# The second scan's elementwise work with one operand in PSUM on VectorE

## The chip, the core and the metric

The kernel runs on one core of a Trainium2 chip. The metric is the device time of one execution in microseconds (us). A core has engines that each work through a queue of their own, in order: TensorE (PE in the profile, its weight loads PEld) multiplies matrices, VectorE (DVE), ScalarE (ACT) and GpSimd (POOL) do the elementwise work, SyncE (SP) starts most transfers. An instruction waits in its queue until what it reads is there and what it overwrites is free; all that stands behind it on that engine waits with it. SBUF is the on-chip memory, PSUM the memory into which TensorE writes and which the other engines can read and write too.

## The reference

Two layers run one after the other on x of 1024 rows by 1024 columns, in float32. The first is a hybrid block (an S5 scan, attention over selected keys, gates). The second is a block of which one half is attention with three dilations and the other half a Mamba-2 scan; their outputs are gated, normalised, joined, multiplied by a matrix and normalised once more. The change lies in the Mamba-2 scan alone. Cut to what matters (16 heads of 64 columns, in 2 groups of 8; 8 chunks of 128 rows; state of 128):

```python
xg = (x * dt[..., None])                      # by chunk
a_cs = jnp.cumsum(dt * a, axis=-1)            # within a chunk
decay = jnp.exp(segsum(adt))                  # exp(a_cs[l] - a_cs[s]), 0 above the diagonal
cb = jnp.einsum('bclgn,bcsgn->bcgls', cc, bc)
y_diag = jnp.einsum('bcgjls,bcsgjp->bclgjp', cb[:, :, :, None] * decay, xg)
decay_to_end = jnp.exp(a_cs[..., -1:] - a_cs)
states = jnp.einsum('bcsgn,bcsgjp->bcgjpn', bc, xg * decay_to_end)
# the states are carried from chunk to chunk: h * chunk_decay + states, prev is h before the chunk
y_off = jnp.einsum('bclgn,bcgjpn->bclgjp', cc, prev) * jnp.exp(a_cs)
y = y_diag + y_off
```

## The kernel before, in words

The program is not written in the order in which it runs. Python generators (tasks) describe the work; a planner (the class `Sched`) plays them in planned time, with a cost for each kind of instruction and a priority for each task, and so fixes the order of each engine's queue. Every instruction is recorded by one helper, so that all of them carry line L280, and a row is told by the names of its tiles. A pair of engines in `yield (G..., V...)` means that the planner takes the one that it thinks is done first. A tile pool hands out a fixed number of buffers: a task that asks for a buffer with none free stands still until one is released.

Most of the time TensorE multiplies: the two large products of each layer (names g<-m,wh and g<-m,wl). A weight block comes by DMA into `raw`, ScalarE rounds it into `wh`, GpSimd takes the rest, `wl = raw - wh`, and TensorE multiplies by both; there are two buffers each of raw, and two pairs of wh and wl (numbers wh_76 with wl_77, wh_78 with wl_79). During the second scan, from about 1089 to 1310 us of the span, these products (the projections of the second layer) fill TensorE between the scan's own matmuls, and their results are read out of PSUM as zp (gates) or go through a convolution on VectorE (names cr, ac, xs).

The scan (`ssd_core`, `chunk`) goes through two groups of heads, first 0, then 1, with the convolution of group 1's inputs between them. For each of the 8 chunks of a group four tasks run beside one another:

- `rows`: four transposes (t<-cst,xs) into a PSUM buffer b, then xg = transposed x times dt, on VectorE.
- `decay`: a DMA fetches R, the cumulated a_cs of 8 heads, to all 128 partitions (R has two buffers); 8 VectorE instructions (E<-R,nacs,cst) make E = R - a_cs plus a mask for each head; ScalarE takes exp; a matmul puts C times B into PSUM (t<-CT,BT), VectorE multiplies E by it (E<-E,t).
- `off`: ScalarE takes exp of R, GpSimd multiplies it by C (R<-R,CT).
- `state`: GpSimd makes xd = xg times the decay to the chunk's end, and the old state times the chunk's decay (pv<-pv,eend); a matmul (s<-xd,Br) makes the chunk's part, VectorE adds it (pv<-pv,s).

Then 16 matmuls (o<-E,xg and o<-R,pv) make the chunk's output, and VectorE adds the skip (xs<-xs,dsk,o, four rows). The buffer of R comes free when these matmuls are done, so the fetch for chunk c+2 starts behind the output of chunk c. `gate_ssm` and `gate_mix` multiply the outputs by the gates and sum their squares (sq<-sq,xs); the task that finishes the eighth block also forms the norm.

Of the kernel before, what the change touches and what calls it, by code (L numbers as in the profile page):

```python
# [311 lines left out]
class Kernel:  # L312
# [5 lines left out]
    def run(self, upto):  # L318
# [12 lines left out]
        def nm(base):  # L331
            cnt[0] += 1
            return f"{base}_{cnt[0]}"
# [41 lines left out]

        cst = pC.tile([128, 912], F32, name="cst")
        ident, tri, cm2 = cst[:, 0:128], cst[:, 128:256], cst[:, 256:512]
        selB, ones, negT = cst[:, 512:640], cst[:, 640:768], cst[:, 768:896]
        eye = cst[:, 896:912]
        gs = pC.tile([128, 16], F32, name="gs")  # L380
        sc = pC.tile([128, 8], F32, name="sc")
# [119 lines left out]
        X = {}  # L501
# [1232 lines left out]
        def gate_mix(u, half, k, done):  # L1734

            r = half * 1024 + k * 128
            yield Q.dma_start(mix_d[r:r + 128], u)
            fire(mix_ev[half][k])
            sq, prev, mine = X["sq"], sq_last[half], Ev()
            sq_last[half] = mine  # L1740
            if prev is None:
                yield A.activation(sq, u, AF.Square)
            else:
                yield A.activation(u, u, AF.Square)
                yield prev
                yield (G.tensor_tensor(sq, sq, u, op=OP.add), V.tensor_tensor(sq, sq, u, op=OP.add))
            fire(mine)
            fire(done)
            count_mix[half] += 1
            if count_mix[half] == 8:  # L1750
                b = yield TB
                yield [P.matmul(b[:, t:t + 1], sq[:, t * 128:(t + 1) * 128], ones[:, 0:1], start=True, stop=True) for t in range(8)]
                ss = X["c2"].tile([128, 8], F32, name=nm("ssm"))
                yield V.tensor_copy(ss, b[:, 0:8])
                release(TB, b)
                rstd[half] = yield from rsqrt(X["c2"], ss, 8, 1.0 / 1024, 1e-5, "m")
                fire(rstd_ev[half])

        count_mix = [0, 0]

# [33 lines left out]
        def ssd_prep():  # L1794
# [33 lines left out]
            yield V.tensor_scalar(X["nacs"], b[:, 0:128], -1.0, None, op0=OP.mult)  # L1828
            yield V.tensor_tensor(X["dec"], b[:, 128:256], X["nacs"], op=OP.add)
            yield A.activation(X["dec"], X["dec"], AF.Exp)  # L1830
            yield A.activation(X["eend"], b[:, 128:256], AF.Exp)
            release(TB, b)
            fire(ssd_ev)
# [88 lines left out]
        def chunk(g, c, xs, prev, pv_ev):  # L1922
# [1 line left out]
            cs = slice(c * 128, (c + 1) * 128)  # L1924
            hs = slice(c * 16 + 8 * g, c * 16 + 8 * g + 8)
            dt2 = X["dt"].rearrange("p c h -> p (c h)")
            xg_ev, e_ev, r_ev = Ev(), Ev(), Ev()
            T = {}

            def bc(ap, n=64):  # L1930
# [2 lines left out]
            def rows():  # L1933
                T["xg"] = yield X["xg"]
                b = yield TB
                yield [P.transpose(b[:, k * 128:(k + 1) * 128], xs[k][:, cs], ident) for k in range(4)]
                yield V.tensor_tensor(T["xg"], b.rearrange("p (h d) -> p h d", h=8), bc(dt2[:, hs]), op=OP.mult)
                release(TB, b)
                fire(xg_ev)

            def decay():

                R = yield X["R"]
                E = yield X["E"]
                T["R"], T["E"] = R, E
                yield Q.dma_start(R, acs_d[hs].rearrange("(o h) l -> o h l", o=1).to_broadcast([128, 8, 128]))
                yield [V.scalar_tensor_tensor(E[:, h], R[:, h], X["nacs"][:, c * 16 + 8 * g + h:c * 16 + 8 * g + h + 1], negT, op0=OP.add, op1=OP.add)
                       for h in range(8)]
                spawn(off(R), 50 + c)
                yield A.activation(E, E, AF.Exp)  # L1950
                b = yield TB
                yield P.matmul(b[:, 0:128], BT[:, cs], CT[:, cs], start=True, stop=True)
                yield V.tensor_tensor(E, E, b[:, None, 0:128].to_broadcast([128, 8, 128]), op=OP.mult)
                release(TB, b)
                fire(e_ev)

            def off(R):
                if c:
                    yield A.activation(R, R, AF.Exp)
                    yield G.tensor_tensor(R, R, CT[:, None, cs].to_broadcast([128, 8, 128]), op=OP.mult)  # L1960
                fire(r_ev)

            def state():
                yield xg_ev
                xd = yield X["xd"]
                yield G.tensor_tensor(xd, T["xg"], bc(X["dec"][:, hs]), op=OP.mult)
                if c:
                    yield pv_ev[c - 1]
                nx = yield X["pv"]
                if c:  # L1970
                    yield G.tensor_tensor(nx, prev[c - 1], bc(X["eend"][:, hs]), op=OP.mult)
                b = yield SB
                sb = b
                yield P.matmul(sb, Br[:, c], xd.rearrange("p h d -> p (h d)"), start=True, stop=True)
                release(X["xd"], xd)
                s3 = sb.rearrange("p (h d) -> p h d", h=8)
                if c:
                    yield V.tensor_tensor(nx, nx, s3, op=OP.add)
                else:
                    yield V.tensor_copy(nx, s3)  # L1980
                release(SB, b)
                prev[c] = nx
                fire(pv_ev[c])
# [354 lines left out]
```

## Time and profile before

| what | value |
|---|---|
| times of the runs | 2014.16, 2019.17, 2019.45 us, median 2019.17 |
| profiled execution | 2019.02 us, its span 2017.3 us |
| mean granted clock of TensorE | 0.989 |
| busy: PE / VectorE / ScalarE / GpSimd | 1937.5 / 1369.6 / 803.8 / 624.9 us |

The span is the time from the first to the last recorded instruction; 1.7 us lie around it. [...] Busy times of different engines overlap. A row's own duration can reach into the next one's, since an engine starts an instruction before the one in front has fully ended. "Idle before" is time in which the engine stood still just before a row, with the engine or transfer that ended it.

### The profile page before, as it was taken

The page shows a single profiled execution, that of the slowest core. Times are in us where ns is not written, and L with a number is a line of the kernel's source. Part 1 is how long each engine was busy: PE and PEld are TensorE (multiplying, and loading weights), DVE is VectorE, ACT ScalarE, POOL GpSimd, SP SyncE. Part 2 cuts the span into 40 slices and gives each one's busy share as a digit, 9 for nine tenths or more (in the row PEclk, how much of TensorE's full clock was granted, in tenths as well). Part 3 has the DMA queues.
Part 4 walks back from the last instruction along what each step waited for, and adds up shares of the span by engine and source line. Part 5 has one row for each costly group of instructions (what it writes and reads, how often), then busy time and mean ns, then how long its engine had stood idle before and what let it go on. Part 6 is the DMA issues. An engine that isn't in the chain of part 4 may idle for free. (4 is left out here: it accounts for less than half of the span.)

```text
span 2017.3 us, 32636 instructions
## 1 busy us (share of the span) xinstructions
PE 1937.5 (96%) x12477; PEld 1634.6 (81%) x12477; DVE 1369.6 (68%) x3203; ACT 803.8 (40%) x1420; POOL 624.9 (31%) x435
## 2 busy tenths in 40 slices
PE   6999999999998999999999899999999999979997
PEld 4777877778887888998887677788889878869997
DVE  5899999986558754635357887746665666684348
ACT  5563322222357742214122333336554555673310
POOL 2215788872300012312223534530100100111233
PEclk9999999999999999999999999999999999989999
DMA  8213466658534134624322334361223311246622
GB/s 287 53 51 86 126 180 166 171 167 274 167 104 152 53 123 139 210 68 114 84 72 83 98 114 128 108 213 53 85 74 92 97 53 64 74 126 196 217 70 84
DMA packets 279004, 245.91 MB, mean 122 GB/s; under 512 B 47376, under 2 KB 230208, under 8 KB 278848
## 3 DMA queue, kind: packets, MB, share of 16 engines
q1 hardware_dynamic: 277696, 239.64, 39.0%
q0 software_dynamic: 1152, 4.19, 0.6%
q8 instruction: 98, 1.61, 0.3%
q14 instruction: 58, 0.48, 0.1%
HBM read 173.46 MB, written 70.32 MB: 121 GB/s over the span
## 5 line engine op out<-in xcount | busy, mean ns | idle before, releaser
L280 POOL TENSOR_TENSOR wl<-raw,wh 128x1024 fp32r<-128x1024 f32 (+3 forms) x140 | 324.3, 2331 | 1098.1 <-ACT wh L280 1001.0
L280 PE MATMUL g<-m,wh 128*128 128x512 f32 x1408 | 449.0, 400 | 0.0
L280 PE MATMUL g<-wh,m 128*128 128x256 f32 (+1 forms) x2048 | 373.0, 284 | 1.1 <-DVE acc L280 0.8
L280 PEld LDWEIGHTS g<-wh,m 128*128 128x128 f32 x2048 | 315.2, 189 | 3.8 <-DVE acc L280 1.2
L280 PEld LDWEIGHTS g<-m,wh 128*128 128x128 f32 x1408 | 258.4, 188 | 58.6 <-issue 5.2
L280 PE MATMUL g<-wl,m 128*128 128x256 f32 (+1 forms) x1024 | 287.7, 281 | 0.0
L280 PE MATMUL g<-m,wl 128*128 128x512 f32 x704 | 278.5, 396 | 4.6 <-POOL wl L280 4.6
L280 ACT ACTIVATE sm<-sm,st 128x1024 f32<-128x1024 f32 (+7 forms) x286 | 213.2, 758 | 73.4 <-DVE st L280 71.2
L280 PE MATMUL g<-hh,wh 128*128 128x512 f32 (+1 forms) x584 | 235.5, 403 | 1.6 <-ACT hh L280 1.6
L280 PE MATMUL g<-hh,wl 128*128 128x512 f32 (+1 forms) x584 | 231.5, 396 | 0.0
L280 PE MATMUL g<-hl,wh 128*128 128x512 f32 (+1 forms) x584 | 230.5, 395 | 1.0 <-DVE hl L280 0.9
L280 ACT ACTIVATE wh<-raw 128x1024 fp32r<-128x1024 f32 (+3 forms) x140 | 132.1, 967 | 221.9 <-PE g L280 97.9
L280 PEld LDWEIGHTS g<-wl,m 128*128 128x128 f32 x1024 | 192.9, 188 | 0.1
L280 PEld LDWEIGHTS g<-m,wl 128*128 128x128 f32 x704 | 132.4, 188 | 35.9 <-POOL wl L280 5.0
L280 PE MATMUL t<-cst,sm 128*128 128x128 f32 x864 | 127.7, 277 | 7.8 <-ACT sm L280 4.5
L280 PEld LDWEIGHTS g<-hh,wh 128*128 128x128 f32 (+1 forms) x584 | 109.5, 187 | 28.9 <-issue 5.1
L280 PEld LDWEIGHTS g<-hh,wl 128*128 128x128 f32 (+1 forms) x584 | 109.3, 187 | 26.6 <-POOL wl L280 0.5
L280 PEld LDWEIGHTS g<-hl,wh 128*128 128x128 f32 (+1 forms) x584 | 109.4, 187 | 24.6 <-DVE hl L280 1.9
L280 PEld LDWEIGHTS t<-cst,sm 128*128 128x128 f32 x864 | 101.0, 142 | 28.3 <-ACT sm L280 10.3
L280 PE MATMUL s<-hf,hf 128*128 128x512 f32 (+2 forms) x384 | 99.1, 371 | 11.0 <-ACT m L280 6.8
L280 DVE COPY sm<-t 128x512 f32<-128x512 f32 (+3 forms) x172 | 92.8, 554 | 12.8 <-PE t L280 10.7
L280 DVE TENSOR_SCALAR_CACHE_REDUCE eq<-score,tk 128x512 f32<-128x512 f32 (+2 forms) x99 | 99.7, 1007 | 0.2
(371 smaller groups left out, 3271.7 us busy)
## 6 DMA issues: line engine op xcount, KB each, us to landing
raw<-in_w_in_dram SPq DMA_DIRECT2D x89, 512.0 KB
raw<-in_w_out_dram SPq DMA_DIRECT2D x24, 512.0 KB
R<-acs_d SPq DMA_DIRECT2D x16, 512.0 KB
tb<-in_tab_dram SPq DMA_DIRECT2D x16, 512.0 KB
wmt<-in_w_mod_dram SPq DMA_DIRECT2D x6, 1024.0 KB
raw<-in_w_mod_dram SPq DMA_DIRECT2D x8, 512.0 KB
q_d<-pj SPq DMA_DIRECT2D x16, 256.0 KB
gb_d<-pj SPq DMA_DIRECT2D x16, 256.0 KB
```

The costliest lines, as they stand in the source:

```text
L280: return Op(self.eng, self.cost(name, a, k) if share is None else share, lambda: fn(*a, **k), name, on_shared_port(self.eng, name, a, k))
```

## The change

All of it is in the second scan. The decay of a chunk is made by two VectorE instructions over all 8 heads, min(R, a_cs) and minus a_cs, with a_cs first copied to 8 columns of PSUM; min bounds the exponent at 0, and the triangle is now masked in the product of C and B (128 by 128 in PSUM, one more instruction). C times exp(R) is made by VectorE, with C copied to PSUM by ScalarE. xd is made by VectorE from the transposes in PSUM, with the decay multiplied by dt beforehand. GpSimd keeps the weights (wl), pv<-pv,eend and some of sq. The norm's last part becomes a task of its own (`mix_rstd`).

```diff
@@ -375,7 +375,7 @@
 
         cst = pC.tile([128, 912], F32, name="cst")
         ident, tri, cm2 = cst[:, 0:128], cst[:, 128:256], cst[:, 256:512]
-        selB, ones, negT = cst[:, 512:640], cst[:, 640:768], cst[:, 768:896]
+        selB, ones = cst[:, 512:640], cst[:, 640:768]
         eye = cst[:, 896:912]
         gs = pC.tile([128, 16], F32, name="gs")
         sc = pC.tile([128, 8], F32, name="sc")
@@ -1748,13 +1748,16 @@
             fire(done)
             count_mix[half] += 1
             if count_mix[half] == 8:
-                b = yield TB
-                yield [P.matmul(b[:, t:t + 1], sq[:, t * 128:(t + 1) * 128], ones[:, 0:1], start=True, stop=True) for t in range(8)]
-                ss = X["c2"].tile([128, 8], F32, name=nm("ssm"))
-                yield V.tensor_copy(ss, b[:, 0:8])
-                release(TB, b)
-                rstd[half] = yield from rsqrt(X["c2"], ss, 8, 1.0 / 1024, 1e-5, "m")
-                fire(rstd_ev[half])
+                spawn(mix_rstd(half, sq), 30)
+
+        def mix_rstd(half, sq):
+            b = yield TB
+            yield [P.matmul(b[:, t:t + 1], sq[:, t * 128:(t + 1) * 128], ones[:, 0:1], start=True, stop=True) for t in range(8)]
+            ss = X["c2"].tile([128, 8], F32, name=nm("ssm"))
+            yield V.tensor_copy(ss, b[:, 0:8])
+            release(TB, b)
+            rstd[half] = yield from rsqrt(X["c2"], ss, 8, 1.0 / 1024, 1e-5, "m")
+            fire(rstd_ev[half])
 
         count_mix = [0, 0]
 
@@ -1828,6 +1831,7 @@
             yield V.tensor_scalar(X["nacs"], b[:, 0:128], -1.0, None, op0=OP.mult)
             yield V.tensor_tensor(X["dec"], b[:, 128:256], X["nacs"], op=OP.add)
             yield A.activation(X["dec"], X["dec"], AF.Exp)
+            yield V.tensor_tensor(X["dec"], X["dec"], dt2, op=OP.mult)
             yield A.activation(X["eend"], b[:, 128:256], AF.Exp)
             release(TB, b)
             fire(ssd_ev)
@@ -1924,7 +1928,7 @@
             cs = slice(c * 128, (c + 1) * 128)
             hs = slice(c * 16 + 8 * g, c * 16 + 8 * g + 8)
             dt2 = X["dt"].rearrange("p c h -> p (c h)")
-            xg_ev, e_ev, r_ev = Ev(), Ev(), Ev()
+            xg_ev, xd_ev, e_ev, r_ev = Ev(), Ev(), Ev(), Ev()
             T = {}
 
             def bc(ap, n=64):
@@ -1935,8 +1939,12 @@
                 b = yield TB
                 yield [P.transpose(b[:, k * 128:(k + 1) * 128], xs[k][:, cs], ident) for k in range(4)]
                 yield V.tensor_tensor(T["xg"], b.rearrange("p (h d) -> p h d", h=8), bc(dt2[:, hs]), op=OP.mult)
+                fire(xg_ev)
+                if c < 7:
+                    T["xd"] = yield X["xd"]
+                    yield V.tensor_tensor(T["xd"], b.rearrange("p (h d) -> p h d", h=8), bc(X["dec"][:, hs]), op=OP.mult)
+                    fire(xd_ev)
                 release(TB, b)
-                fire(xg_ev)
 
             def decay():
 
@@ -1944,26 +1952,33 @@
                 E = yield X["E"]
                 T["R"], T["E"] = R, E
                 yield Q.dma_start(R, acs_d[hs].rearrange("(o h) l -> o h l", o=1).to_broadcast([128, 8, 128]))
-                yield [V.scalar_tensor_tensor(E[:, h], R[:, h], X["nacs"][:, c * 16 + 8 * g + h:c * 16 + 8 * g + h + 1], negT, op0=OP.add, op1=OP.add)
-                       for h in range(8)]
+                b = yield TB
+
+                cb, na = b[:, 128:256], b[:, 256:264]
+                yield V.tensor_scalar(na, X["nacs"][:, hs], -1.0, None, op0=OP.mult)
+
+                yield V.tensor_tensor(E, R, na[:, :, None].to_broadcast([128, 8, 128]), op=OP.min)
                 spawn(off(R), 50 + c)
+                yield V.tensor_tensor(E, E, na[:, :, None].to_broadcast([128, 8, 128]), op=OP.subtract)
                 yield A.activation(E, E, AF.Exp)
-                b = yield TB
                 yield P.matmul(b[:, 0:128], BT[:, cs], CT[:, cs], start=True, stop=True)
-                yield V.tensor_tensor(E, E, b[:, None, 0:128].to_broadcast([128, 8, 128]), op=OP.mult)
+                yield V.tensor_tensor(cb, b[:, 0:128], tri, op=OP.mult)
+                yield V.tensor_tensor(E, E, cb[:, None, :].to_broadcast([128, 8, 128]), op=OP.mult)
                 release(TB, b)
                 fire(e_ev)
 
             def off(R):
                 if c:
                     yield A.activation(R, R, AF.Exp)
-                    yield G.tensor_tensor(R, R, CT[:, None, cs].to_broadcast([128, 8, 128]), op=OP.mult)
+                    b = yield TB
+                    yield A.activation(b[:, 0:128], CT[:, cs], AF.Copy)
+                    yield V.tensor_tensor(R, R, b[:, None, 0:128].to_broadcast([128, 8, 128]), op=OP.mult)
+                    release(TB, b)
                 fire(r_ev)
 
             def state():
-                yield xg_ev
-                xd = yield X["xd"]
-                yield G.tensor_tensor(xd, T["xg"], bc(X["dec"][:, hs]), op=OP.mult)
+                yield xd_ev
+                xd = T["xd"]
                 if c:
                     yield pv_ev[c - 1]
                 nx = yield X["pv"]
```

The planner's order changes with it, only from 1089 to about 1340 us of the span. TensorE has as many instructions as before. At the end of group 0, on TensorE (m are rows of the layer's input, _69 and _7413 buffer numbers; o<-E_7881 is the output of the last chunk), the queue was:

```order
L280 MATMUL g_69<-m_7413,wh_76 128x512
L280 MATMUL g_69<-m_7414,wh_76 128x512
L280 MATMUL g_69<-m_7413,wl_77 128x512
L280 MATMUL o_75<-E_7881,xg_7877 64x128 x2
L280 MATMUL o_75<-R_7879,pv_7883 64x128 x2
L280 MATMUL o_75<-E_7881,xg_7877 64x128 x2
L280 MATMUL o_75<-R_7879,pv_7883 64x128 x2
L280 MATMUL o_75<-E_7881,xg_7877 64x128 x2
L280 MATMUL o_75<-R_7879,pv_7883 64x128 x2
L280 MATMUL o_75<-E_7881,xg_7877 64x128 x2
L280 MATMUL o_75<-R_7879,pv_7883 64x128 x2
L280 MATMUL g_69<-m_7413,wh_76 128x512
```

and is now:

```order
L280 MATMUL o_75<-E_7880,xg_7876 64x128 x2
L280 MATMUL o_75<-R_7878,pv_7884 64x128 x2
L280 MATMUL t_74<-cst,xs_7874 128x128
L280 MATMUL t_74<-cst,xs_7875 128x128
L280 MATMUL t_74<-cst,xs_7872 128x128
L280 MATMUL t_74<-cst,xs_7873 128x128
L280 MATMUL s_71<-xd_7882,Br 128x512
L280 MATMUL t_73<-CT,BT 128x128
L280 MATMUL o_75<-E_7881,xg_7877 64x128 x2
L280 MATMUL o_75<-R_7879,pv_7883 64x128 x2
L280 MATMUL o_75<-E_7881,xg_7877 64x128 x2
L280 MATMUL o_75<-R_7879,pv_7883 64x128 x2
```

Before, four groups of g stood between the output of chunk 6 and that of chunk 7; now the last transposes, a state and one C times B stand there, and no g; those g follow the last output instead.

On GpSimd, between the two groups (the first wl pair is for weights used at the start of the stretch, the second for those at its end), the queue was:

```order
L280 TENSOR_TENSOR wl_77<-raw_81,wh_76 128x8x128
L280 TENSOR_TENSOR wl_77<-raw_80,wh_76 128x8x128
L280 TENSOR_TENSOR sq<-sq,xs_7875 128x1024
L280 TENSOR_TENSOR sq<-sq,xs_7872 128x1024
L280 TENSOR_TENSOR sq<-sq,xs_7873 128x1024
L280 TENSOR_TENSOR wl_79<-raw_81,wh_78 128x8x128
L280 TENSOR_TENSOR wl_79<-raw_80,wh_78 128x8x128
```

and is now:

```order
L280 TENSOR_TENSOR pv_7884<-pv_7883,eend 128x512
L280 TENSOR_TENSOR pv_7883<-pv_7884,eend 128x512
L280 TENSOR_TENSOR wl_77<-raw_81,wh_76 128x8x128
L280 TENSOR_TENSOR wl_77<-raw_80,wh_76 128x8x128
L280 TENSOR_TENSOR sq<-sq,xs_7875 128x1024
L280 TENSOR_TENSOR sq<-sq,xs_7872 128x1024
L280 TENSOR_TENSOR wl_79<-raw_81,wh_78 128x8x128
L280 TENSOR_TENSOR wl_79<-raw_80,wh_78 128x8x128
```

Of the three sums of squares the last has gone to VectorE, so that the second pair of wl stands one row earlier; ahead of the first pair pv<-pv,eend remains of the chunks' work.

On VectorE, in the last chunk of group 0 (E_7881 and R_7879 are its decay, t_73 and t_74 its PSUM buffers), the queue was:

```order
L280 SCALAR_TENSOR_TENSOR E_7881<-R_7879,nacs,cst 128x128 x8
L280 TENSOR_TENSOR xg_7877<-t_73,dt 128x512
L280 TENSOR_TENSOR E_7880<-E_7880,t_74 128x1024
L280 SCALAR_TENSOR_TENSOR zp_6758<-zp_6758,g_68 128x512
L280 SCALAR_TENSOR_TENSOR xs_7874<-xs_7874,dsk_7868,o_75 128x128
L280 SCALAR_TENSOR_TENSOR xs_7875<-xs_7875,dsk_7868,o_75 128x128
L280 SCALAR_TENSOR_TENSOR xs_7872<-xs_7872,dsk_7868,o_75 128x128
L280 TENSOR_TENSOR pv_7883<-pv_7883,s_71 128x512
L280 SCALAR_TENSOR_TENSOR xs_7873<-xs_7873,dsk_7868,o_75 128x128
L280 TENSOR_TENSOR E_7881<-E_7881,t_73 128x1024
```

and is now:

```order
L280 TENSOR_TENSOR E_7881<-R_7879,t_73 128x1024
L280 SCALAR_TENSOR_TENSOR zp_6759<-zp_6759,g_69 128x512
L280 TENSOR_TENSOR E_7881<-E_7881,t_73 128x1024
L280 SCALAR_TENSOR_TENSOR xs_7874<-xs_7874,dsk_7868,o_75 128x128
L280 TENSOR_TENSOR xg_7877<-t_74,dt 128x512
L280 SCALAR_TENSOR_TENSOR xs_7875<-xs_7875,dsk_7868,o_75 128x128
L280 TENSOR_TENSOR pv_7883<-pv_7883,s_71 128x512
L280 SCALAR_TENSOR_TENSOR xs_7872<-xs_7872,dsk_7868,o_75 128x128
L280 TENSOR_TENSOR R_7879<-R_7879,t_74 128x1024
L280 SCALAR_TENSOR_TENSOR xs_7873<-xs_7873,dsk_7868,o_75 128x128
L280 TENSOR_TENSOR t_73<-t_73,cst 128x128
L280 TENSOR_TENSOR E_7881<-E_7881,t_73 128x1024
```

Behind the fetch of R stood eight narrow rows, eight others and the product; now twelve rows stand there, four of them 1024 columns wide, and R times C is one of them.

## Rows read from the trace of the kernel before

**Rows 1.** Busy time by stretch: each engine's busy us (rows), granted clock, DMA share, GB/s

```profile
1089.00:1169.80 80.80, 73.80 (x495) 57.44 (x494) 63.40 (x128) 23.16 (x27) 39.56 (x24) 0.98 0.33 107
1169.80:1237.30 67.50, 62.95 (x271) 50.61 (x271) 57.86 (x40) 22.97 (x29) 27.82 (x9) 0.97 0.38 117
1237.30:1310.00 72.70, 71.72 (x495) 55.95 (x494) 58.89 (x129) 23.46 (x27) 39.64 (x24) 1.00 0.38 120
```

**Rows 2.** Waits of PE, first and second stretch of rows 1: total us, times, longest

```profile
PE o L280 <- DVE E L280: 6.2, 4, 2.8
...
PE g L280 <- POOL wl L280: 4.6, 1, 4.6
```

**Rows 3.** VectorE's groups by shape, 1085 to 1310: busy us, mean ns | idle before

```profile
L280 DVE SCALAR_TENSOR_TENSOR E<-R,nacs,cst 128x128 f32<-128x128 f32 x128 | 55.6, 503 | 12.6 <-DMA R<-acs_d 12.4
...
L280 DVE TENSOR_TENSOR E<-E,t 128x1024 f32<-128x1024 f32 x16 | 19.4, 1212 | 0.9 <-issue 0.4
L280 DVE SCALAR_TENSOR_TENSOR xs<-xs,dsk,o 128x128 f32<-128x128 f32 x64 | 19.2, 341 | 9.7 <-PE o L280 9.7
...
L280 DVE TENSOR_TENSOR xg<-t,dt 128x512 f32<-128x512 f32 x16 | 10.7, 682 | 4.8 <-PE t L280 4.8
...
L280 DVE SCALAR_TENSOR_TENSOR xs<-xs,ac 128x1024 f32<-128x1024 f32 x4 | 4.9, 1226 | 4.1 <-ACT xs L280 4.1
...
L280 DVE TENSOR_TENSOR dec<-t,nacs 128x128 f32<-128x128 f32 x1 | 0.3, 291 | 0.0
```

**Rows 4.** The same view, 1335 to 1341: a row eight columns wide

```profile
L280 DVE TENSOR_SCALAR nv<-ssm 128x8 f32<-128x8 f32 x1 | 0.2, 171 | 0.0
```

**Rows 5.** Timeline of VectorE: start, us, engine, operation, count, idle before

```profile
1108.81 2.19 DVE L280 SCALAR_TENSOR_TENSOR E<-R,nacs,cst 128x128 f32<-128x128 f32 x8 [1.32 <-DMA R<-acs_d]
...
1126.16 2.19 DVE L280 SCALAR_TENSOR_TENSOR E<-R,nacs,cst 128x128 f32<-128x128 f32 x8 [2.52 <-DMA R<-acs_d]
...
1130.87 6.04 DVE L280 SCALAR_TENSOR_TENSOR E<-R,nacs,cst 128x128 f32<-128x128 f32 x8
```

**Rows 6.** Timeline of GpSimd beside the last of rows 5

```profile
1130.36 2.42 POOL L280 TENSOR_TENSOR R<-R,CT 128x1024 f32<-128x1024 f32 x1
1132.73 2.45 POOL L280 TENSOR_TENSOR wl<-raw,wh 128x1024 fp32r<-128x1024 f32 x1
```

**Rows 7.** Timeline of SyncE's queue: two fetches of R

```profile
1102.54 0.68 SPq L280 DMA_DIRECT2D R<-acs_d  x1
...
1122.54 4.52 SPq L280 DMA_DIRECT2D R<-acs_d  x2
```

**Rows 8.** Timeline of PE, late in the second group

```profile
1296.22 0.44 PE L280 MATMUL o<-E,xg 128*64 128x128 f32 x4
...
1298.11 0.66 PE L280 MATMUL t<-cst,xs 128*128 128x128 f32 x4
...
1299.31 0.63 PE L280 MATMUL g<-m,wh 128*128 128x512 f32 x2
...
1300.01 1.02 PE L280 MATMUL s<-xd,Br 128*128 128x512 f32 x2
```

**Rows 9.** Timeline of PE at the wait between the groups

```profile
1209.23 0.79 PE L280 MATMUL g<-m,wl 128*128 128x512 f32 x1 [4.55 <-POOL wl L280]
```

**Rows 10.** Timeline of GpSimd between the groups

```profile
1171.67 5.97 POOL L280 TENSOR_TENSOR wl<-raw,wh 128x1024 fp32r<-128x1024 f32 x2 [12.48 <-ACT wh L280]
...
1203.05 2.85 POOL L280 TENSOR_TENSOR sq<-sq,xs 128x1024 f32<-128x1024 f32 x1 [5.78 <-ACT xs L280]
1205.85 6.64 POOL L280 TENSOR_TENSOR wl<-raw,wh 128x1024 fp32r<-128x1024 f32 x2
```

**Rows 11.** Timeline of VectorE between the groups

```profile
1172.48 2.90 DVE L280 SCALAR_TENSOR_TENSOR xs<-zl,xs 128x512 f32<-128x512 f32 x1
1175.30 3.42 DVE L280 SCALAR_TENSOR_TENSOR ac<-cr,cw,ac 128x1024 f32<-128x1024 f32 x1
```

**Rows 12.** Timeline of ScalarE between the groups

```profile
1202.81 1.99 ACT L280 ACTIVATE wh<-raw 128x1024 fp32r<-128x1024 f32 x2
```

## The prediction

> **What bounds the kernel now.** I read the busy shares first: TensorE is busy for 96% of the span, so only its idle time and its slowed clock can be won. The order of the instructions differs only between 1089 and about 1340 us, so I then read the busy times by stretch there, and for each stretch the waits of TensorE. The first stretch is group 0 of the scan, the second the convolution between the groups, the third group 1. TensorE stands idle for 80.8 - 73.8 = 7.0 us in the first, 67.5 - 62.95 = 4.55 in the second and 72.7 - 71.72 = 0.98 in the third [rows 1]. The clock granted was 0.98 and 0.97 in the first two and 1.00 in the third [rows 1]; the missing share is 0.02 x 80.8 = 1.6 us and 0.03 x 67.5 = 2.0 us of work. In all 12.5 + 3.6 = 16.1 us are at stake, 0.8% of the time.
>
> The waits have two causes. In group 0 four waits for E on VectorE make 6.2 of the 7.0 us, the longest 2.8; between the groups one wait for wl on GpSimd makes all 4.6 [rows 2]. Behind both stand VectorE and GpSimd holding each other up. Eight rows that make E take 2.19 us when GpSimd is still, and 6.04 while it multiplies R by C (2.42) and makes a wl (2.45) [rows 5, 6]; over the scan their mean is 503 ns against 2.19 / 8 = 274 [rows 3, 5]. A row that reads PSUM shows nothing of it: xg is at 682 ns in the mean, with GpSimd busy beside many of them [rows 3].
>
> **The change part by part**, against the profiled execution of 2019.02 us (span 2017.3, 1.7 around it; 0.15 below the median of 2019.17).
>
> *VectorE in a chunk.* Eight rows for E go (8 x 0.503 = 4.0 us with the collisions, 2.19 without). In come: a_cs to 8 columns of PSUM, not in the trace; nearest a row of 128 by 8 in SBUF at 0.171 [rows 4] and one of 128 by 128 from PSUM at 0.291 [rows 3], I take 0.2. Two rows of 1024 columns (min, minus): nearest E<-E,t, which has one operand in PSUM too, at 1.212 [rows 3]. The operand is repeated along the columns here, but xg repeats one too and costs no more for its width. I take 1.21 each; the ends are, for both together, the 2.19 of the eight rows and 2 x 1.23 (two operands in SBUF, xs<-xs,ac) [rows 3, 5]. The masked product of C and B: 0.291 by the row dec<-t,nacs [rows 3]. R times C: as E<-E,t, 1.21. xd: as xg, 0.68 [rows 3]. In a train a row costs about 0.07 less than it lasts (274 against 341 ns for the same width [rows 3, 5]). A group so has 30 rows of 512 columns (xg, xd, pv, zp) at 0.61, 31 of 1024 at 1.14, 32 skips at 0.27, 8 each at 0.22 and 0.2: 18.3 + 35.3 + 8.6 + 1.8 + 1.6 = 65.6 us, 8.2 a chunk. TensorE's own work in group 0 is 80.8 - 7.0 - 1.6 = 72.2, 9.0 a chunk. So VectorE is no longer held up, but it has 0.8 us a chunk to spare and no more. What counts is where the end of the chain falls.
>
> *The end of group 0.* The fetch of the last R starts when the output of chunk 5 is done, since R has two buffers. It lands in 3.6 us (1122.54 to 1126.16 [rows 5, 7]); where weight blocks were fetched beside it, in 6.3 (1102.54 to 1108.81). Then the twelve rows of the order go one by one: 1.21 (min) + 0.61 + 1.14 + 0.27 + 0.61 + 0.27 + 0.61 + 0.27 + 1.14 (R) + 0.27 + 0.25 + 1.21 (E) = 7.9 us; ScalarE's two exponentials lie beside the rows between. With 0.2 for the hand-over, 3.6 + 7.9 + 0.2 = 11.7 from the end of output 5 to the start of output 7. TensorE has in that time five groups of g at 0.70 (1299.31 to 1300.01), output 6 at 1.9 (1296.22 to 1298.11), four transposes at about 0.5, a state at 0.9 and two C times B at 0.2 each [rows 8]: 3.5 + 1.9 + 0.5 + 0.9 + 0.4 = 7.2. It waits for 4.5. Before, four groups of g lay between outputs 6 and 7 and the longest wait was 2.8 [rows 2]. To this I add 2.0 for smaller waits in the chunks ahead (0.8 us to spare a chunk, but fetches of 3.6 to 6.3; between 0 and 7.0 - 2.8 = 4.2), and 1.5 for the clock, as before: 8.0, against 8.6. Gain 0.6; ends: 8.6 if nothing waits, and -5 if both, the wait and the fetch, are long.
>
> *Between the groups.* The wait of 4.55 ends when the first wl of 1205.85 is done [rows 9, 10]. What it reads, wh, came as the first of two rows at 1202.81 [rows 12], so about 1203.8; GpSimd then had the third sum of squares, 1203.05 to 1205.85. That has left its queue: wl starts 2.05 earlier. The pair of wl at 1171.67 met VectorE's rows at 1172.48 and 1175.30, which took 2.90 and 3.42 [rows 10, 11] where their like take 0.68 (as xg) and 1.23 (as xs<-xs,ac) [rows 3]: 4.3 us of delay for the chain of the convolution, which ends in that wh. The pair now stands ahead of group 0's end, so this goes. Against it, TensorE comes 2.8 us earlier in relation to the scan's end, as four groups of g stand behind the last output. So 4.55 - 2.05 - 4.3 + 2.8 = 1.0 remains, and with so short a wait the slow clock (2.0) goes too: gain 6.55 - 1.0 = 5.5, at least -1 if the wl pair meets other rows, at most 6.55.
>
> *Group 1.* It loses 0.98 now [rows 1]; its last output comes 39 TensorE instructions later than before. VectorE's longer rows and the last fetch give it a part of what group 0 has: I take 2.0, loss 1.0, between 1 gained and 7 lost (as group 0).
>
> *At nothing.* ScalarE's copy of C (14 rows; ScalarE is busy for 23 of 81 us [rows 1]), the one row dec times dt, and the norm as a task of its own: they lie beside TensorE's products. If their cover were gone, the copies would add 0.3 each to the chain of R, which is shorter than that of E by the rows between. GpSimd's 14 products of R and 14 of xd go from an engine that nobody but wl waits for.
>
> [...] E<-E,t, with one operand in PSUM, takes 1.212 us, xs<-xs,ac of the same width with both in SBUF 1.226 [rows 3]: PSUM costs nothing extra here. [...]
>
> Sum: 0.6 + 5.5 - 1.0 = 5.1 us; 2019.0 - 5.1 = 2013.9.
>
> **The rivals.**
> 1. *The ends are hidden too.* The planner lets the last fetches and rows come early, and group 0 loses only 2 instead of 8 us. For it: group 1 lost only 0.98 with the same kind of chunks. Against it: the order puts no g between outputs 6 and 7. 2013.9 - 6 = 2008.
> 2. *The gap between the groups stays.* GpSimd and VectorE meet there as before (three sums of squares and two pairs of wl beside the convolution), the change doing nothing for the weights. For it: the convolution's rows still have all operands in SBUF. Against it: the sum that stood in front is gone from the queue. 2013.9 + 5.5 = 2019.4, no change.
> 3. *Rows with an operand in PSUM do not overlap with the next one*, and cost 0.07 more each than I count. About 20 VectorE rows stand in the two last chains: 1.4 us; in a chunk it is under the 0.8 to spare. For it: the 0.07 was read from rows of 128 columns. Against it: nothing in these rows. 2013.9 + 1.4 = 2015.3.
> 4. *Slower: the fetch of R stops VectorE's queue.* min stands in front of other chunks' rows (pv, R times C, xs), and all wait with it. With 6.3 us for a fetch instead of 3.6, 2.7 come to each chunk; it decides from the 0.8 to spare. Then 12 of 16 chunks lose 2.7 - 0.8 = 1.9, 23 us, plus a last wait of 4.5 in each group, 9, against the 16.1 lost now: +16, 2035. For it: VectorE waits for R already, 12.4 us over the scan [rows 3]. Against it: the fetch was 3.6 in quiet places, and it is issued a chunk ahead.
>
> **How the numbers follow.** A difference of 0.3%, 6.1 us, is about what a measurement of this kernel can tell from no change: faster is below 2013.1. Chances: forecast 0.42, rival 1 0.20, rival 2 0.20, rival 3 0.08, rival 4 0.10. The forecast's own range is 2009 to 2018 and puts 0.45 of itself below 2013.1; rival 1 lies below, rivals 2 and 3 nearly all within. So faster 0.42 x 0.45 + 0.20 + 0.04 = 0.43; slower 0.10 with a little of rival 2, 0.11; the same 0.46. The range of 2004 to 2022 leaves out rival 4 and the ends of rival 1.
>
> **What would show it.** In the profile after: VectorE's 1024-column rows for E at 1.2 us and no 6 us trains; a wait of TensorE for E of 4 to 5 us ahead of group 0's last output; the wait for wl between the groups at about 1 us; wl rows near 2.4 us in the scan. I am wrong if the waits for E exceed 10 us in a group, if the wl wait is still over 3 us, or if a wait appears in the stretches after 1340 us, where the order is the same.

## The result, and the profile after

The changed kernel takes 2034.05 us (median of 4 runs, 2028.84 to 2035.24) against 2019.31 of the kernel before in the same runs: ratio 1.0073, 95% interval 1.0059 to 1.0087, 14.7 us slower. The forecast was 2013.9 in a range of 2004 to 2022. The profiled execution has a span of 2033.4 us, 16.1 more than before.

The busy times of the changed kernel by stretch answer to [rows 1]: group 0 to the end of its last output, the convolution, group 1 to the end of its last output, from there to the first row of the attention stage (hf<-g), and 40 us behind it. (The third stretch of [rows 1] ends at 1310.0, 4 us behind the last output.)

```profile
1089.00:1167.70 78.70, 73.44 (x495) 57.34 (x493) 64.85 (x105) 27.70 (x37) 20.45 (x12) 0.96 0.37 120
1167.70:1236.30 68.60, 64.43 (x277) 51.73 (x274) 54.95 (x46) 20.08 (x25) 18.54 (x6) 0.97 0.32 104
1236.30:1312.10 75.80, 75.62 (x513) 59.27 (x511) 65.32 (x106) 26.05 (x35) 15.72 (x10) 1.00 0.37 119
1312.10:1362.00 49.90, 36.09 (x147) 29.37 (x144) 22.01 (x33) 10.80 (x14) 13.36 (x5) 0.79 0.66 216
1362.00:1402.00 40.00, 40.00 (x223) 32.74 (x222) 24.83 (x67) 22.26 (x41) 4.78 (x2) 1.00 0.10 27
```

TensorE's waits from 1089 to 1400 answer to [rows 2] (total us, times, longest):

```profile
PE t L280 <- DVE sq L280: 13.8, 1, 13.8
PE o L280 <- DVE E L280: 4.5, 2, 4.3
PE g L280 <- ACT cr L280: 4.2, 1, 4.2
PE t L280 <- DVE E L280: 1.0, 1, 1.0
```

Up to group 1's last output the change is a small gain. The loss is in the fourth stretch. Before, the same part of the program had no wait and the full clock:

```profile
1305.90:1346.10 40.20, 40.20 (x183) 32.90 (x183) 19.55 (x33) 11.17 (x14) 14.50 (x6) 1.00 0.67 218
```

It ends with the first hf row, before and now:

```profile
1346.14 0.59 ACT L280 ACTIVATE hf<-g 64x512 fp32r<-64x512 f32 x1 [3.06 <-PE g L280]
```

```profile
1361.99 0.59 ACT L280 ACTIVATE hf<-g 64x512 fp32r<-64x512 f32 x1 [13.44 <-PE g L280]
```

TensorE now stands for 13.8 us for sq, and the granted clock of the stretch is 0.79. From the end of the last output to the first hf row TensorE has 39 instructions less than before (they stand ahead of the output now), 9.0 us at 0.23 each (three rows of g in 0.70 [rows 8]). Before, this part took 1346.1 - 1305.9 = 40.2 us, so it should take 31.2 and takes 49.9: 18.7 lost, of which 13.8 is the wait and 4.9 the slow clock behind it. The clock by itself: it was granted at 0.50 in the later part of the wait and in 9.65 us of work behind it, of which half, 4.8, would be lost, an estimate from that share. In the rows, three of g take 1.28 us there (1354.71 to 1355.99) against 0.71 at 1.00 (1359.68 to 1360.39), and the sixteen of the norm 3.57 against 1.84 before.

```profile
1339.00:1349.85 10.85, 0.00 (x0) 0.00 (x0) 4.27 (x3) 1.91 (x2) 5.24 (x2) 0.50 0.67 205
1349.85:1359.50 9.65, 9.65 (x31) 8.29 (x32) 2.19 (x13) 0.00 (x0) 0.00 (x0) 0.50 0.95 312
```

The last output came 2.8 us earlier than its 39 additional instructions would put it (1312.1 against 1305.9 + 9.0); 18.7 - 2.8 = 15.9, by which the first hf row is late (1361.99 against 1346.14).

The row that waits is the norm of the scan's half: sixteen matmuls that add up the columns of sq. TensorE was ready for them at 1336.0 (the end of the first row):

```profile
1335.65 0.40 PE L280 MATMUL g<-m,wl 128*128 128x512 f32 x1
1349.85 3.57 PE L280 MATMUL t<-cst,sq 128*128 128x1 f32 x16 [13.81 <-DVE sq L280]
```

What they wait for is a chain of the last four blocks (gates, store, square, sum). Its VectorE rows, with the wl pairs of GpSimd from 1315.49 (5.39 us) and 1338.98 (5.25 us) beside the first and the third:

```profile
1315.10 3.50 DVE L280 SCALAR_TENSOR_TENSOR xs<-zl,xs 128x512 f32<-128x512 f32 x2
...
1333.25 3.49 DVE L280 SCALAR_TENSOR_TENSOR xs<-zl,xs 128x512 f32<-128x512 f32 x2
...
1339.20 2.84 DVE L280 SCALAR_TENSOR_TENSOR xs<-zl,xs 128x512 f32<-128x512 f32 x1
1348.58 1.23 DVE L280 TENSOR_TENSOR sq<-sq,xs 128x1024 f32<-128x1024 f32 x1 [6.53 <-ACT xs L280]
```

Its last store in SyncE's queue, behind a weight block, and the square on ScalarE that waits until the store has read its block:

```profile
1341.52 0.38 SPq L280 DMA_DIRECT2D raw<-in_w_in_dram  x1
1342.07 0.46 SPq L280 DMA_DIRECT2D mix_d<-xs  x1
```

```profile
1347.49 1.06 ACT L280 ACTIVATE xs<-xs 128x1024 f32<-128x1024 f32 x1 [7.63 <-DMA mix_d<-xs]
```

The chain is full of slow hops: 3.50 us for two rows that take 1.34 elsewhere in it, 2.84 for one of 0.69, and 5.4 us from the issue of the store to the square. Slow hops were there before too: two rows xs<-zl,xs took 3.51 us (at 1317.79), and the last store took 3.8 from its issue (1328.74) to the square (1332.51), so that of its 5.4 us 1.6 are new. From the end of the last output to the end of sq the chain takes 37.6 us (1312.2 to 1349.8); before it took 29.0 (1305.9 to 1334.9), and TensorE came to the norm at 1335.1, 0.2 us later:

```profile
1333.68 1.23 DVE L280 TENSOR_TENSOR sq<-sq,xs 128x1024 f32<-128x1024 f32 x1 [3.92 <-ACT xs L280]
```

```profile
1335.10 1.84 PE L280 MATMUL t<-cst,sq 128*128 128x1 f32 x16
```

At the end of group 0, the fetch of the last R, the first VectorE row behind it and the output that waits:

```profile
1151.32 0.32 SPq L280 DMA_DIRECT2D R<-acs_d  x1
```

```profile
1156.45 1.22 DVE L280 TENSOR_TENSOR E<-R,t 128x1024 f32<-128x1024 f32 x1 [2.43 <-DMA R<-acs_d]
```

```profile
1164.28 0.69 PE L280 MATMUL o<-E,xg 128*64 128x128 f32 x4 [4.27 <-DVE E L280]
```

Between the groups the wait for wl is gone, and one for ScalarE's cr stands in its place:

```profile
1208.83 0.84 PE L280 MATMUL g<-m,wh 128*128 128x512 f32 x2 [4.17 <-ACT cr L280]
```

GpSimd's wl pair, VectorE's convolution and ScalarE's queue there:

```profile
1198.45 6.28 POOL L280 TENSOR_TENSOR wl<-raw,wh 128x1024 fp32r<-128x1024 f32 x2 [7.05 <-ACT wh L280]
```

```profile
1199.16 7.98 DVE L280 SCALAR_TENSOR_TENSOR ac<-cr,cw,ac 128x1024 f32<-128x1024 f32 x3
...
1210.51 3.92 DVE L280 SCALAR_TENSOR_TENSOR ac<-cr,cw,ac 128x1024 f32<-128x1024 f32 x3
```

```profile
1199.22 0.58 ACT L280 ACTIVATE cr<-g 128x512 f32<-128x512 f32 x1
1207.24 1.06 ACT L280 ACTIVATE xs<-ac 128x1024 f32<-128x1024 f32 x1 [7.43 <-DVE ac L280]
1208.20 0.58 ACT L280 ACTIVATE cr<-g 128x512 f32<-128x512 f32 x1
```

Three rows ac, with all operands in SBUF, take 7.98 us beside the wl pair and 3.92 without. The tanh xs<-ac waits for them, and behind it in ScalarE's queue stands the copy cr<-g that empties TensorE's PSUM buffer.

The rows of VectorE, 1085 to 1330, answer to [rows 3]:

```profile
L280 DVE TENSOR_TENSOR E<-E,t 128x1024 f32<-128x1024 f32 x32 | 38.9, 1217 | 0.7
...
L280 DVE TENSOR_TENSOR E<-R,t 128x1024 f32<-128x1024 f32 x16 | 19.5, 1220 | 10.4 <-DMA R<-acs_d 10.0
L280 DVE TENSOR_TENSOR R<-R,t 128x1024 f32<-128x1024 f32 x14 | 17.0, 1216 | 0.0
...
L280 DVE TENSOR_TENSOR xd<-t,dec 128x512 f32<-128x512 f32 x14 | 9.6, 685 | 0.0
...
L280 DVE TENSOR_TENSOR t<-t,cst 128x128 f32<-128x128 f32 x16 | 4.7, 295 | 0.1
L280 DVE TENSOR_SCALAR t<-nacs 128x8 f32<-128x8 f32 x16 | 2.6, 162 | 0.0
```

### The profile page after: what moved, and what is told of

Its sections match the earlier page's. It is cut to its first block, busy times and chain, and to the rows that moved or that the text cites. A ratio compares the mean times of both kernels' runs of the same rounds, so it can differ in the third digit from the quotient of the medians.

```text
span 2033.4 us, 32582 instructions
## 1 busy us (share of the span) xinstructions
PE 1942.3 (96%) x12477; PEld 1638.8 (81%) x12477; DVE 1383.0 (68%) x3171; ACT 807.1 (40%) x1433; POOL 570.8 (28%) x405
## 4 chain that ended last, share of the span: by engine, by line
PE 73%; DVE 11%; DMA 6%; POOL 3%; ACT 3%; issue 2%; SPq 1%; DVEq 0%; POOLq 0%; ACTq 0%
PE g L280 53%; PE s L280 8%; PE o L280 6%; PE t L280 6%; DMA raw<-in_w_in_dram 2%; DVE eq L280 1%; POOL wl L280 1%; DVE acc L280 1%; DVE sm L280 1%; DVE ac L280 1%; DVE jk L280 1%; SPq L280 1%; DMA zp<-mix_d 1%; ACT sm L280 1%; DVE xs L280 1%
```

## The experiments

All are measured against the kernel before, in the same runs (its medians: 2017.6, 2019.18 and 2017.69 us in the three sets). "Distance" is the number of places in TensorE's order from the last matmul of the scan's last output to the first of the norm's. Before it is 127, in the changed kernel 103.

**The norm later** (the changed kernel with one number):

```diff
         def mix_rstd(half, sq):
+            if half:
+                yield 16.0
             b = yield TB
```

> The changed kernel with one number added: the task of the second scan's norm starts 16 planned us later, so that its 16 small matmuls (t<-cst,sq) stand 72 instructions later in TensorE's queue; the order of TensorE's other instructions is unchanged. Theory A (the loss is the place of these matmuls: they stand in TensorE's queue before their sum of squares is ready, and all behind them waits): the wait of 13.8 us goes to under 3, the clock after it stays near 1.00, the first hf row comes 10 to 15 us earlier than the 1361.99 of the changed kernel, and the time is 2017 to 2023 us. Theory B (VectorE has too much work in the scan, and the wait is only where it shows): the wait moves to another row behind the scan, and the time stays at 2030 to 2036.

2016.2 us, ratio 0.9986 (0.9977 to 0.9996): by the ratios 17.5 us less than the changed kernel, more than the whole loss, as theory A says of the cause; the time is 0.8 below its range. The chain is as long as ever, but TensorE does not wait for it; it does the norm 2.6 us behind its sum (1348.82 + 1.23 to 1352.70), and the granted clock is 1.00 from 1312 to 1362. The first hf row comes 13.3 us earlier, and no more, since on ScalarE it stands behind the last square (1347.73, 1.06 us), which still waits for its store. The first scores of the attention stage (sm<-s,tb on VectorE) come 18.4 us earlier, at 1364.18 against 1382.58:

```profile
1352.70 1.84 PE L280 MATMUL t<-cst,sq 128*128 128x1 f32 x16
```

```profile
1348.70 0.58 ACT L280 ACTIVATE hf<-g 64x512 fp32r<-64x512 f32 x1
```

```profile
1364.18 0.69 DVE L280 CUSTOM_DVE_ANT_0 sm<-s,tb 128x512 f32<-128x512 f32 x1 [1.30 <-PE s L280]
```

and in the changed kernel:

```profile
1382.58 0.69 DVE L280 CUSTOM_DVE_ANT_0 sm<-s,tb 128x512 f32<-128x512 f32 x1 [1.29 <-PE s L280]
```

The other waits are still there (longest first, 1085 to 1365):

```profile
PE g L280 <- ACT cr L280: 4.5, 1, 4.5
PE o L280 <- DVE E L280: 4.3, 1, 4.3
PE t L280 <- DVE R L280: 0.5, 1, 0.5
```

**The control**: the same later norm in the kernel before (there as the task `mix_rstd` too).

> The kernel before, with the norm as a task of its own that starts 16 planned us later, as in the earlier run on the changed kernel (TensorE's matmuls for it stand 69 instructions later). A control: before, these matmuls waited for nothing (the sum of squares was done 0.2 us ahead of them). Theory A (the changed kernel lost by the wait for sq, and a later norm helps only by taking that wait away): no change against before, 2016 to 2021. Rival: a later norm gains by itself, by some other effect on what follows: 2005 to 2012.

2017.98 us, ratio 1.0000 (0.9991 to 1.0009). A later norm gains nothing where nothing waited for it.

**The square aside** (the changed kernel):

```diff
-                yield A.activation(u, u, AF.Square)
+                v = u
+                if half and k > 3:
+                    v = yield X["ac"]
+                yield A.activation(v, u, AF.Square)
                 yield prev
-                yield (G.tensor_tensor(sq, sq, u, op=OP.add), V.tensor_tensor(sq, sq, u, op=OP.add))
+                yield (G.tensor_tensor(sq, sq, v, op=OP.add), V.tensor_tensor(sq, sq, v, op=OP.add))
+                if v is not u:
+                    release(X["ac"], v)
```

> The changed kernel with the squares of group 1's four blocks written to the convolution's idle buffer and not in place, so that a square no longer waits until its block's store to mix_d has been read out. The places of the norm's matmuls and of the last output are unchanged. Theory C (that store, 5.4 us from its issue at 1342.07 to the square at 1347.49, is what makes the chain long): the wait for sq falls by 4 to 6 us to 8 to 10, the time to 2027 to 2031. Theory A alone says the same for this hop and no more: the remaining wait is still there, as the chain has other late hops. If the stores are hidden behind other hops the wait stays at 12 to 14 and the time at 2032 to 2036.

2032.58 us, ratio 1.0062 (1.0045 to 1.0078). The wait for sq fell by 5.9 to 7.9 us, so the store is one of the slow hops. The time fell by 1.5 us only, to a value above the expected 2027 to 2031, and the intervals of the two kernels overlap. In its profiled execution group 1 began 2.9 us later (1239.18 against 1236.26; the wait for cr was 0.6 longer), the first scores come 3.5 us earlier (1379.04 against 1382.58), and of these 1.5 are lost again behind them, where the order is the same (span 2031.4 against 2033.4). It is not settled why group 1 began later and what cost these 1.5.

**R times C on GpSimd again** (the changed kernel with this one part undone):

```diff
                     yield A.activation(R, R, AF.Exp)
-                    b = yield TB
-                    yield A.activation(b[:, 0:128], CT[:, cs], AF.Copy)
-                    yield V.tensor_tensor(R, R, b[:, None, 0:128].to_broadcast([128, 8, 128]), op=OP.mult)
-                    release(TB, b)
+                    yield G.tensor_tensor(R, R, CT[:, None, cs].to_broadcast([128, 8, 128]), op=OP.mult)
```

> The changed kernel with one part undone: R times C is on GpSimd again (all else as changed). The order then has 139 TensorE instructions between the end of the last output and the norm's matmuls (103 in the changed kernel, 127 before). Theory A: at about 0.235 us each that is 32.7 us, enough for a chain of 28 to 34: the wait for sq is 0 to 3 us, the time 2015 to 2022. Theory B: VectorE has lost 17 us of its work in the scan, so the time falls as well, but by the waits for E (5.5 us in the changed kernel) and not by the one for sq, to 2026 to 2030. Theory C (the store of the last block before it is squared makes the chain long): the wait stays above 8 us, 2028 to 2034.

2002.52 us, ratio 0.9921 (0.9908 to 0.9934): faster than expected of any theory. The order of the whole scan changes with the edit. The distance is 139, the norm waits for nothing, and no other wait of the scan is left but this:

```profile
PE o L280 <- DVE E L280: 0.2, 1, 0.2
```

**R times C on VectorE alone** (the kernel before with that part of the diff).

> The kernel before with one part of the change alone: R times C on VectorE with C in PSUM. The order has 88 TensorE instructions between the last output and the norm's matmuls, 20.7 us. Theory A: with a chain of 28 to 36 us the wait for sq is 7 to 15 us, and the time 2026 to 2036, as bad as the whole change. Theory B: VectorE has here 17 us more work in the scan and the eight-row decay besides, the waits for E grow, 2024 to 2032, with no wait for sq above 3. If neither holds, 2017 to 2021.

2034.02 us, ratio 1.0074 (1.0058 to 1.0090): as large a loss as that of the whole change comes with this part alone, and in this kernel the norm is not a task of its own, so that the new task is not what costs. With a distance of 88 the wait for sq is 7.6 us, as theory A has it. Theory B as it stands (no wait for sq above 3) does not hold, but waits for VectorE and GpSimd come on top: for R (4.7), E (3.6), wl (2.3), zp (1.2) and xg (0.6).

**What of that product costs: VectorE's row or the PSUM buffer.** Two edits of the changed kernel, the row without the buffer (off_sbuf) and the buffer without the row (off_hold):

```diff
-                    b = yield TB
-                    yield A.activation(b[:, 0:128], CT[:, cs], AF.Copy)
-                    yield V.tensor_tensor(R, R, b[:, None, 0:128].to_broadcast([128, 8, 128]), op=OP.mult)
-                    release(TB, b)
+                    yield V.tensor_tensor(R, R, CT[:, None, cs].to_broadcast([128, 8, 128]), op=OP.mult)
...
-                    yield V.tensor_tensor(R, R, b[:, None, 0:128].to_broadcast([128, 8, 128]), op=OP.mult)
+                    yield G.tensor_tensor(R, R, CT[:, None, cs].to_broadcast([128, 8, 128]), op=OP.mult)
```

> The changed kernel with R times C still on VectorE, but with C read from SBUF: ScalarE's copy is gone and no PSUM buffer is asked for. VectorE's row of 1024 columns stays (about 1.22 us, two operands in SBUF). Two theories of what in the product on VectorE costs the 31 us between the changed kernel (2034) and the one with this product on GpSimd (2002.5). Theory V (VectorE's time: 14 rows, 17 us, in the queue ahead of E): nothing is better, the wait for sq stays at 6 us or more and the time is 2024 to 2036. Theory P (the PSUM buffer: there are two of this kind, and the product holds one while transposes, C times B and the columns of a_cs wait for one): most of it comes back, 2002 to 2012. In the order the last output is at 5879 and the norm at 5991, 112 apart (103 in the changed kernel), which leaves a wait for sq of some 5 us in either case if the chain keeps its 36 us.

> The changed kernel with R times C on GpSimd as before, but with a PSUM buffer taken for it, filled by ScalarE's copy of C and held until GpSimd's row (about 2.4 us) is done; the copy is read by nobody. Theory P (the PSUM buffer): as slow as the changed kernel or worse, 2026 to 2038, with a wait for sq of over 6 us. Theory V (VectorE's time): close to the kernel that has the product on GpSimd and no buffer, 2001 to 2008, with no such wait.

2021.30 us, ratio 1.0009 (1.0001 to 1.0018), and 2021.72, ratio 1.0012 (1.0001 to 1.0023). Both theories are missed: by the ratios each edit has some 18 us more than the kernel with the product on GpSimd, the changed kernel 31. The edits are not clean halves. Without the buffer ScalarE's copy is gone too, and the row has two operands in SBUF; it takes 1.385 us in the mean, against 1.216 with C in PSUM:

```profile
L280 DVE TENSOR_TENSOR R<-R,CT 128x1024 f32<-128x1024 f32 x14 | 19.4, 1385 | 0.0
```

Without the row the buffer is held while GpSimd multiplies (2.392 us in the mean in the kernel before, about twice VectorE's 1.216). TensorE's waits show where the time goes. The row without the buffer:

```profile
PE t L280 <- DVE sq L280: 8.0, 1, 8.0
PE o L280 <- DVE E L280: 4.1, 2, 3.8
```

and the buffer without the row:

```profile
PE t L280 <- DVE sq L280: 7.6, 1, 7.6
PE g L280 <- DVE zp L280: 2.8, 1, 2.8
PE g L280 <- POOL wl L280: 2.3, 1, 2.3
PE o L280 <- DVE E L280: 0.4, 1, 0.4
```

In both the distance is 112 and the wait for sq about 8 us. The wait for E at the end of group 0 goes with the order: in the changed kernel no rows of g stand between the last two outputs of group 0 (wait 4.3), in off_sbuf three (3.8), in off_hold fifteen (none; its 0.4 is at the first output of group 1, at 1247.85). The kernel with R times C on VectorE alone has twenty-four there and no such wait (its 3.6 is at the first output of group 0, at 1102.51). So the row on VectorE does not by itself make this wait.

**The decay alone, xd alone** (the kernel before with the one or the other part of the diff).

> The kernel before with the decay alone made in the new way (min and minus over 8 heads, a_cs in PSUM, the triangle in C times B). In the order 142 TensorE instructions stand between the last output and the norm's matmuls (127 before). Theory A (the place of the norm) allows no wait for sq above 2 us. The eight-row trains of up to 6 us go, and with them most of the 7.0 us of waits for E: 2005 to 2013. If the gain of decay and xd together (15 us) needs both, 2010 to 2018.

> The kernel before with xd alone moved to VectorE (from the transposes in PSUM). 130 TensorE instructions between the last output and the norm: no wait for sq above 2 us. The eight rows of E still meet R times C and wl on GpSimd, so waits for E remain, 3 to 7 us: 2012 to 2020.

2005.88 us, ratio 0.9936 (0.9919 to 0.9952), distance 142, with one wait left, for cr, 2.4 us. And 2012.11 us, ratio 0.9961 (0.9946 to 0.9976), distance 130, with 3.3 for E and 0.7 for sq. Both parts gain by themselves.

**The tanh later** (the changed kernel with the later norm, and in the convolution's tail):

```diff
+            yield 3.0
             yield A.activation(dst, ac, AF.Tanh)
```

> The changed kernel with the later norm (2016.2 us) and one number more: the tanh of the convolution is planned 3 us later, so that between the groups ScalarE's copy cr<-g, which frees TensorE's PSUM buffer, stands ahead of a tanh that waits for three slow rows on VectorE, and not behind it. Theory D (the wait of 4.2 to 4.5 us for cr between the groups is ScalarE's order): that wait goes below 1.5 us and the time falls by 4 to 7 us, to 2009 to 2013. Rival (VectorE is late there in any case, by the collision with the wl pair): the wait moves to another row of the same stretch and the time stays at 2014 to 2019.

2001.83 us, ratio 0.9918 (0.9903 to 0.9933), 14.4 us below the later norm alone, three times what was expected of it. The wait for cr is gone, as theory D says. So is that for E at the end of group 0: the new order has twelve rows of g between the last two outputs there, which the expectation had not looked at. The edit does more than move one tanh: TensorE's order changes in many places of the scan, and beside the wl pair there now stand other rows of VectorE (the pair at 1187.56, three rows ac at 1194.31 in 3.93 us). So the run shows that the wait can be planned away, and not that ScalarE's order by itself made it. One wait is left:

```profile
PE t L280 <- DVE R L280: 1.1, 1, 1.1
```

This kernel does all that the change does, the product of R and C on VectorE included. It beats both kernels, as does the one with that product on GpSimd; the two can't be told apart. The later tanh was not tried in the kernel before.

The waits of TensorE from 1085 to 1365 us, summed, beside the profiled spans:

| kernel | distance | waits, us | of it for sq | span, us |
|---|---|---|---|---|
| tanh later | 166 | 1.1 | 0 | 1999.4 |
| R times C on GpSimd | 139 | 0.2 | 0 | 2000.6 |
| decay alone | 142 | 2.4 | 0 | 2004.9 |
| xd alone | 130 | 4.0 | 0.7 | 2006.4 |
| norm later | 175 | 9.3 | 0 | 2014.4 |
| before with the later norm | 196 | 10.9 | 0 | 2014.6 |
| before | 127 | 12.4 | 0 | 2017.3 |
| buffer without the row | 112 | 13.1 | 7.6 | 2020.2 |
| row without the buffer | 112 | 12.1 | 8.0 | 2021.9 |
| R times C on VectorE alone | 88 | 20.0 | 7.6 | 2028.7 |
| the square aside | 103 | 18.2 | 7.9 | 2031.4 |
| changed | 103 | 23.5 | 13.8 | 2033.4 |

Each span is one execution. From the first scores to the end, where the order is the same in all, the executions take between 650.0 us (tanh later, 1349.38 to 1999.4) and 654.0 (decay alone, 1350.88 to 2004.9), so that differences of a few us between rows are not to be read as the scan's.

## Why the prediction was wrong

- *What bounds the kernel*: right. TensorE's idle time and its clock in this part of the program make up most of the differences, as the table shows, though not row by row: from the first row to the last it is 22.4 us more of waits and 34 us more of span. In the last row 17.1 us of TensorE's work ran at the lower clock (4.0 at the end of group 0, 3.4 between the groups, 9.65 behind the norm), so half of it, 8.5, is put as lost, by the estimate above; in the first row the granted clock of all of these stretches was 1.00.
- *VectorE in a chunk*: right in its prices. The rows of 1024 columns take 1.217 to 1.220 us (1.21 taken), the masked product 0.295 (0.291), the columns of a_cs 0.162 (0.2), and the long trains are gone. An operand in PSUM costs nothing in the changed kernel either: xs<-xs,ac, of 1024 columns with both operands in SBUF, takes 1.225 there.
- *The end of group 0*: the size came out, in part by luck. The wait was 4.3 us for a predicted 4.5. The twelve rows took 7.8 us (1156.45 to 1164.22) for a predicted 7.9. But the fetch took 5.1 us from its issue to the first of them for a predicted 3.6; against that TensorE had 7.8 us of work in between for 7.2, and a wait of 1.0 ahead of the last C times B. The term for smaller waits was 2.0 and came to that 1.0. Of the clock 2.0 us were lost, by the same estimate, for a predicted 1.5 (0.50 in the 4.0 us of work from 1164.28 to 1168.30; the mean of 0.96 counts the wait too). In all 78.7 - 73.4 + 2.0 = 7.3 us were lost for a predicted 8.0; before, by the same reading (0.51 from 1157.5 to 1160.9), 7.0 + 1.7 = 8.7.
- *Between the groups*: the wait for wl went, as worked out, but a gain of 5.5 was forecast and about 0.1 came: 4.2 of waiting and half of 3.4 us of work at the lower clock (0.50 from 1209.3 to 1212.7), 5.9 together, against 4.55 and half of 2.9 (1209.23 to 1212.10, at 0.50), 6.0. The step failed at "The pair now stands ahead of group 0's end, so this goes". That is true of the first wl pair. The second then met the convolution, and the chain from VectorE by the tanh to ScalarE's cr, which frees PSUM, was not followed. (The delay there, 2.90 - 0.68 and 3.42 - 1.23, is 4.4 and not 4.3, which changes nothing.)
- *Group 1*: forecast as a loss of 1.0; it waits for 0.2 us (75.8 - 75.6), 0.8 less than before. With the two stretches ahead (8.7 - 7.3 and 0.1) the gain up to the last output is 2.3 us, near the 2.8 by which the last output came earlier.
- *At nothing*: this is the step that decided the sign. It put "the norm as a task of its own" beside TensorE's products. The task itself does cost nothing: the control has it and is as fast as the kernel before, and R times C on VectorE alone loses as much without it. But its matmuls stand in TensorE's own queue, in the order, and the sentence never asked when sq is done against when TensorE comes there. Before, the margin was 0.2 us (1334.9 and 1335.1). The order put the last output 39 instructions later and the norm only 15, which takes 24 x 0.23 = 5.5 us from the chain; the chain itself took 37.6 us for 29.0. 5.5 + 8.6 - 0.2 = 13.9, against a measured wait of 13.8; with the slow clock behind it that is 18.7 us for a term put at 0. "Its last output" 39 instructions later was in the text, under group 1, and nothing followed from it.
- *The rivals*: the slower one gave 2035 by the fetch of R in VectorE's queue. Its number came out by luck; that is not what happened: VectorE waits 10.0 us for R, 12.4 before [rows 3].
- *The signs of being wrong*: the waits for E stayed under 10 us and the wait for wl went, so two of the three did not come. The third did: a wait that reaches beyond 1340 us (1336.05 to 1349.85).

Why the planner brings the norm so near to the last output when R times C is on VectorE or holds a buffer was not settled; the runs show only that the distance is 112 and less in the kernels that do so in the planner's own order, and 127 and more in the others. Nor was it settled what of the chain's 8.6 us is due to which hop, beyond the 1.6 of the last store.

## What to carry to other kernels

Where a planner fixes the queues, a change of costs or engines can move all that is planned behind it. Look up, on the engine that bounds the kernel, every instruction whose input comes from a chain of other engines, and compare its new place with the chain's measured length, not the planned one. A margin of 0.2 us in the trace, as here, can be gone with the next order. Before a change is judged, the same work should be tried with one or two places in the order moved: here the whole change is 0.7% slower as planned and 0.8% faster with two numbers more. Of these two the later norm gave the kernel before nothing; the later tanh was not tried there, so how much of the 0.8% belongs to the change is not shown.

## What the runs showed of the hardware

TensorE stood from 1336.05 to 1349.85; the granted clock fell from 1.00 to 0.50 at 1339.0, within the wait, and rose to 1.00 at 1359.5, among the products behind the norm. The sixteen small matmuls took 3.57 us there, at 0.50, against 1.84 in the kernel before, at 1.00. So the wait cost more than its length, here 18.7 us for 13.8.

Three rows ac of 1024 columns with all operands in SBUF took 7.98 us beside GpSimd's wl pair and 3.92 without it. R times C on VectorE took 1.216 us in the mean with C in PSUM and 1.385 with C in SBUF, with a median of 1.219 and a longest row of 2.623: in these runs the operand in PSUM cost nothing, and the rows that had one stayed at their length (in the changed kernel 1.210 to 1.221 for R times C and 1.209 to 1.222 for E<-E,t).
